# When block 2's memory is opened: at the third-last group of block 1, or at its last

## The chip, the cores and the metric

The kernel runs on one core of a Trainium2 chip. The metric is the device time of one execution in microseconds (us); where several runs are given, their median. The engines named below are PE (matrix multiply), DVE (vector), ACT (activation functions), POOL (a second, slower vector engine) and SP, whose queue issues nearly all DMA transfers.

## The reference

One transformer layer over 2048 positions of width 1024, in float32:

```
hn   = rms_norm(x, attn_norm_g);  proj = hn @ w_in        # q,k,v of 4 heads, gated linear attention, pooling
a    = diff_attention(q, k, v, lam, bias)                  # causal: block i of the queries sees keys 0..i
b, c = gated linear attention, multiscale pooling
h    = x + concat(a, b, c) @ w_out                         # output projection
hn   = rms_norm(h, ffn_norm_g)
out  = h + (silu(hn @ w_gate) * (hn @ w_up)) @ w_down      # FFN, hidden width 2816
```

## The kernel before

Every float32 matrix is split into a high and a low part, and each product is made of three matmuls (high by high, high by low, low by high). The positions are cut into four blocks of 512 (b = 0 to 3).

The first stage makes all projections and starts on attention. The second stage is the FFN, and it is the stage of this change. It walks over `steps`: for each block b, groups g = 0 to 10 (`NG` = 11), each group two slices of 128 of the hidden width (`GS` = 2). A group of blocks 0 and 1 is gate and up of its first slice (`first`, 48 matmuls of 512 columns), the down projection of the group before it (`down`, 48 matmuls), and gate and up of its second slice (`second`, 48 matmuls). The matmuls of `gate_up` and of `oproj` stand in `tile24`, at L1310 to L1312; those of `down` in the helper `mm`, at L133.

Blocks 2 and 3 do gate and up in another way. `unit` makes the product of a group by a scheme of seven products of half the size in place of eight (L1382, matmuls of 256 columns, 84 for a unit; a group has a unit "G" and a unit "U"). For that the normalised block has to be turned into seven operands first, named B11, T2, T1, B21, T3, B22 and T4, each in high and low parts. `tprep(b)` does this on DVE, ACT and POOL: it waits for the row scales of the block (`rowscale2`, which needs the last result of the output projection), normalises (L1245), forms sums and differences (L1250 to L1264), and splits them (L1239 on ACT, L1240 on DVE or POOL). The first products of a unit are made with B11, then T2, T1 and B21.

Beside this "left" stream of dense work runs a "right" stream, the attention of blocks 1 to 3 (`rside`). Both are Python generators; after each piece of dense work `tick` lets the right stream issue four steps (`RT2` = 4.0). So most of attention is issued between dense matmuls. At step (1, NG-3), group 8 of block 1, the line `until(lambda: not rside)` issues all that is left of attention in one piece. Only then its memory can be reused: the region `pp` is opened (one more weight buffer, three work buffers, half of block 2's rows), five more PSUM banks go to the dense stream, and block 2's mixed rows are loaded (`mixes(2)`) into X[2] and X[3], which held the keys and values of attention.

Weights pass through a ring of 2048-column buffers (`wring`; four of them in this stage until `pp` adds a fifth). `pieces` is the list of weight pieces in the order in which they are asked for, and `oplace` says at which step the output projection of a block stands: block 2's at (1, NG-1), before the gate and up of the last group of block 1.

The order that the code issues is not quite the order that runs: a scheduler in the build fixes each engine's order, by its own estimate, and moves independent work forward. Each engine then works through its list in order, so an instruction that waits holds up all behind it on that engine. SP's queue is in order as well.

Of the kernel before, what the change touches and what calls it, by code (L numbers as in the profile page):

```python
# [20 lines left out]
KT = D // P  # L21
BLK = 512
NB = S // BLK
NF = 2816 // P
# [3 lines left out]
GS = 2  # L28
# [59 lines left out]
def body(nc, tc, V, G, ACT, PE, DMA, A, banks, dram):  # L88
    side, rside = [], []
    rate = [0.0, 0.0]  # L90
    def spawn(g):

        if g is not None:
            side.append(g)
            advance([g], side)
# [41 lines left out]
    X = [C.view(4096, R) for i in range(4)]  # L137
# [288 lines left out]
    pieces = []  # L426
# [7 lines left out]
    NG = NF // GS  # L434
    steps = [(b, g) for b in range(NB) for g in range(NG)]

    def oplace(b, g):

        return {(0, 0): 0, (1, 0): 1, (1, NG - 1): 2, (2, 3): 3}.get((b, g))

    keep = {}

    def kept(k, i):

        if (k, i) not in keep:
            keep[k, i] = dram(f"wk{k}{i}", [P, 2048])
        return keep[k, i]

    def dpiece(b, fi):
        return (("d", b, fi), kept("d", fi), A["w_d"][fi], -2 if b else 0)  # L450

    for n, (b, g) in enumerate(steps):
        ob = oplace(b, g)
        if ob == 1:
            pieces += [dpiece(0, NF - GS + q) for q in range(2)]
        if ob is not None:
            pieces += [(("o", ob, d), kept("o", d), A["w_o"][d], -2 if ob else 0) for d in range(KT)]
        for i in range(2):
            if b < 2:
                fi = GS * g + i  # L460
                for k in "gu":
                    pieces.append(((k, b, fi), kept(k, fi) if b == 1 else None, A["w_" + k][fi], 0))
            else:
                pieces += [(("GU"[i], b, g), q, A[("w_g", "w_u")[i]][GS * g + q], -1) for q in range(2)]
            if i == 0 and n and ob != 1:
                pb, pg = steps[n - 1]
                pieces += [dpiece(pb, GS * pg + q) for q in range(2)]
    pieces += [dpiece(NB - 1, NF - GS + q) for q in range(2)]
# [618 lines left out]
    for si, (half, k, b) in enumerate(seq):  # L1087
        kind, i = UN[k]
# [25 lines left out]
        else:  # L1114
            n = 272 if i == 2 else 256
# [37 lines left out]
    fring = p2.ring(4, 1024, R)  # L1153
# [8 lines left out]
    def getw(key):  # L1162
        while key not in W2:
            pump()
            tick()
        return W2[key]

    def relw(key):
        wrel(W2.pop(key)[2])

    xs = [(r3(X[2 * q], KT), r3(X[2 * q + 1], KT)) for q in range(2)] + [None]
    ready = {}
# [285 lines left out]
    def down(b, g, ds):  # L1458
        grp = range(GS * g, GS * g + GS)
        dw = [getw(("d", b, fi)) for fi in grp]  # L1460
        for d in ds:
            until(lambda: all((fi, b) in fft for fi in grp))
            bank = force(dense.acq())
            prs = []
            for fi, (dH, dL, _) in zip(grp, dw):
                fH, fL, _ = fft[(fi, b)]
                prs += [(dH[:, d, :], fH), (dH[:, d, :], fL), (dL[:, d, :], fH)]
            mm(bank, prs)
            spawn(ch_down(d, b, bank, g == NG - 1))
            if d % 2:  # L1470
                pump()
            tick()
        if d == KT - 1:
            for fi in grp:
                fring.rel(fft.pop((fi, b))[2])
                relw(("d", b, fi))
# [17 lines left out]

    mixes(0)
    for n, (b, g) in enumerate(steps):
        if (b, g) == (1, NG - 3):
            until(lambda: not rside)
            dense.rel(*sbank.free, obank.free.pop())
            sbank.free.clear()  # L1500
            pp = Region(tc, "pp")
            wring.rel(pp.view(2048, R))
            tr2.rel(*[pp.view(528) for _ in range(3)])
            h2[2] = [pp.view(BLK) for _ in range(4)] + ht[4:8]
            acc2.append(pp.view(BLK))
            mixes(2)
        ob = oplace(b, g)
        if ob == 1:
            down(0, NG - 1, range(4))
        if ob is not None:  # L1510
            oproj(ob)
        if ob == 1:
            down(0, NG - 1, range(4, KT))
        if ob == 2:
            ready[("Xa", 2)] = True
            spawn(tprep(2))
        if (b, g) == (2, 1):
            until(lambda: ready.get(("Tall", 2)))
            mx = Region(tc, "mx", "right")
            xs[2] = (r3(mx.view(4096, R), KT), r3(mx.view(4096, R), KT))  # L1520
            mixes(3)
        if ob == 3:
            mx.close()
            lend()
        if (b, g) == (2, NG - 3):
            claim()
        if (b, g) == (2, NG - 1):
            until(lambda: len(back) == 3)
            wx.pop().close()
            spawn(tprep(3))  # L1530
        first(b, g)
        split = b != 1 and g == NG - 1
        if n and ob != 1:
            down(*steps[n - 1], range(4 if split else KT))
        second(b, g)
        if (b, g) == (1, NG - 1):
            ready[("Xb", 2)] = True
            fring.rel(X[1][:, 2048:3072], X[1][:, 3072:4096])
        if (b, g) == (2, NG - 1):
            ready[("Xa", 3)] = ready[("Xb", 3)] = True  # L1540
        if (b, g) == (0, NG - 1):
            mixes(1)
        if split:
            down(*steps[n - 1], range(4, KT))
# [85 lines left out]
```

## Time and profile before

| what | us |
|---|---|
| median of 3 runs (2691.2 to 2696.0) | 2693.79 |
| the profiled execution | 2695.36 |
| its span in the trace | 2693.6 |
| PE busy in the span | 2546.4 (95%) |
| DVE busy | 1932.9 (72%) |
| ACT busy | 1193.8 (44%) |
| POOL busy | 905.8 (34%) |

The profiled execution took 1.8 us beyond its span and is 1.6 us above the median. The page's second part cuts the span into 40 slices of 67 us and gives each engine's busy share in tenths, so one can see at once where PE is not full; a row below it gives the clock that PE was granted.

### The profile page before, as it was taken

The numbers are of one execution on the slowest core, as the hardware profiler recorded it, in microseconds if no ns is written. First come the engines' busy times: TensorE is split into PE (matmuls) and PEld (weight loads), VectorE is DVE, ScalarE is ACT, GpSimd is POOL, SyncE is SP. The second block draws the span as 40 slices with busy tenths as digits, with TensorE's granted clock in tenths as the row PEclk, the third lists the DMA queues.
The fourth block names the chain that finished last, engine by engine and source line by source line (L and its number), as shares of the span: only waits on it lengthen the run. The fifth ranks groups of instructions, "written<-read, shape, count | busy, mean of one in ns | idle before, by whom it ended". The sixth has DMA issues, their size and how long they took to land.

```text
span 2693.6 us, 39021 instructions
## 1 busy us (share of the span) xinstructions
PE 2546.4 (95%) x14064; PEld 2170.0 (81%) x14064; DVE 1932.9 (72%) x4002; ACT 1193.8 (44%) x2275; POOL 905.8 (34%) x595
## 2 busy tenths in 40 slices
PE   7998889989899999999999999779999999999999
PEld 5886778868778888877788887567788999899998
DVE  7769886689678787875767677752773678766665
ACT  3555645356554544444444354441342333433332
POOL 4326432355734343322322212011323332423332
PEclk8999989999999999999999999789999999999999
DMA  5333645336755545566776757327586665676664
GB/s 167 123 111 112 188 138 159 106 102 209 259 175 163 183 137 174 153 216 198 250 237 223 245 198 250 83 78 257 182 297 243 261 239 179 231 266 225 242 252 171
DMA packets 185518, 517.52 MB, mean 192 GB/s; under 512 B 19067, under 2 KB 63660, under 8 KB 158700
## 3 DMA queue, kind: packets, MB, share of 16 engines
q1 hardware_dynamic: 185036, 515.00, 56.8%
q8 instruction: 111, 1.82, 0.3%
q14 instruction: 83, 0.68, 0.1%
q10 hardware_dynamic: 288, 0.02, 0.0%
HBM read 386.10 MB, written 128.84 MB: 191 GB/s over the span
## 4 chain that ended last, share of the span: by engine, by line
PE 72%; DVE 16%; DMA 4%; issue 4%; ACT 3%; POOL 2%; SPq 0%; DVEq 0%; POOLq 0%; ACTq 0%
PE bk L133 29%; PE bk L1382 14%; PE bk L1312 7%; PE bk L1310 7%; PE bk L1311 7%; PE bk L1106 2%; PE bk L1107 2%; PE bk L1108 2%; PE bk L986 2%; DVE at L961 1%; DMA at<-qd 1%; DVE p L1347 1%; DVE c L249 1%; DVE at L941 1%; ACT at L953 1%
## 5 line engine op out<-in xcount | busy, mean ns | idle before, releaser
L133 PE MATMUL bk<-p,c 128*128 128x512 f32 x1184 | 323.2, 398 | 11.5 <-DVE p L217 3.9
L1310 PE MATMUL bk<-c,c 128*128 128x512 f32 x664 | 266.8, 403 | 5.6 <-DMA c<-wko 3.2
L1312 PE MATMUL bk<-c,c 128*128 128x512 f32 x664 | 265.3, 400 | 1.8 <-POOL c L542 1.7
L1311 PE MATMUL bk<-c,c 128*128 128x512 f32 x664 | 266.5, 402 | 0.0
L133 PEld LDWEIGHTS bk<-p,c 128*128 128x128 f32 x1184 | 218.0, 190 | 58.2 <-DVE p L217 4.3
L953 ACT ACTIVATE at<-at,at 128x1024 f32<-128x1024 f32 (+4 forms) x192 | 171.6, 895 | 172.0 <-DVE at L950 171.8
L542 POOL TENSOR_TENSOR c<-c,c 128x1024 fp32r<-128x1024 f32 x58 | 143.4, 2475 | 244.0 <-ACT c L541 198.0
L1347 DVE TENSOR_TENSOR p<-p,bk 128x512 f32<-128x512 f32 x308 | 203.6, 680 | 27.4 <-PE bk L133 26.8
L941 DVE TENSOR_SCALAR_CACHE_REDUCE at<-bk 128x512 f32<-128x512 f32 (+3 forms) x304 | 154.5, 521 | 93.8 <-PE bk L133 92.2
L133 PE MATMUL bk<-c,c 128*128 128x256 f32 (+2 forms) x1344 | 206.5, 302 | 9.3 <-DVE p L393 3.7
L133 PE MATMUL bk<-c,at 128*128 128x512 f32 (+4 forms) x704 | 188.2, 364 | 25.3 <-DMA at<-qd 12.4
L1106 PE MATMUL bk<-c,c 128*128 128x512 f32 x448 | 183.8, 412 | 18.9 <-ACT c L554 9.4
L1382 PE MATMUL bk<-c,c 128*128 128x256 f32 x1488 | 196.7, 283 | 4.0 <-POOL c L493 1.9
L133 PEld LDWEIGHTS bk<-c,c 128*128 128x128 f32 x1344 | 181.5, 190 | 20.6 <-DVE p L393 4.7
L1382 PEld LDWEIGHTS bk<-c,c 128*128 128x128 f32 x1488 | 187.9, 190 | 8.0 <-POOL c L493 2.3
L1107 PE MATMUL bk<-c,c 128*128 128x512 f32 x448 | 184.1, 411 | 5.9 <-DVE c L250 5.7
L1108 PE MATMUL bk<-c,c 128*128 128x512 f32 x448 | 182.0, 406 | 1.4 <-DVE c L555 1.4
L133 PEld LDWEIGHTS bk<-c,at 128*128 128x128 f32 x704 | 120.8, 195 | 57.2 <-DVE at L941 26.6
L1310 PEld LDWEIGHTS bk<-c,c 128*128 128x128 f32 x664 | 126.2, 190 | 35.6 <-DMA c<-wko 3.7
L1312 PEld LDWEIGHTS bk<-c,c 128*128 128x128 f32 x664 | 126.2, 190 | 31.0 <-POOL c L542 2.7
L1311 PEld LDWEIGHTS bk<-c,c 128*128 128x128 f32 x664 | 126.3, 190 | 28.1 <-DVE c L1182 0.3
L133 PE MATMUL bk<-at,c 128*128 128x256 f32 (+1 forms) x856 | 143.9, 289 | 1.9 <-DVE at L991 0.7
(378 smaller groups left out, 5912.9 us busy)
## 6 DMA issues: line engine op xcount, KB each, us to landing
c<-wkd SPq DMA_DIRECT2D x38, 1024.0 KB, 6.5
c<-w_u SPq DMA_DIRECT2D x56, 512.0 KB, 5.8
c<-w_g SPq DMA_DIRECT2D x55, 512.0 KB, 5.8
wkg<-c SPq DMA_DIRECT2D x19, 1024.0 KB, 4.9
c<-kd SPq DMA_DIRECT2D x72, 256.0 KB, 5.0
c<-vd SPq DMA_DIRECT2D x72, 256.0 KB, 3.9
c<-wko SPq DMA_DIRECT2D x17, 1024.0 KB, 5.4
p<-w_g SPq DMA_DIRECT2D x33, 512.0 KB, 5.3
```

The costliest lines, as they stand in the source:

```text
L133: PE.matmul(out, l, r, start=start and i == 0, stop=stop and i == n - 1)
L542: G.tensor_tensor(wL, raw[:, :1024], f(wH), op=ALU.subtract)
L941: V.tensor_scalar(p[:, c0:c0 + far], pt[:, :far], 1.0, None, op0=ALU.mult, op1=ALU.max, accum_out=mx[:, nx:nx + 1])
L953: ACT.activation(p[:, c0:c1], p[:, c0:c1], AF.Exp, bias=nmx, accum_out=u.z[:, i, m, k:k + 1])
L1106: PE.matmul(bank, wH[:, kt, :], hH[:, kt, :], start=st, stop=False)
L1107: PE.matmul(bank, wH[:, kt, :], hL[:, kt, :], start=False, stop=False)
L1108: PE.matmul(bank, wL[:, kt, :], hH[:, kt, :], start=False, stop=sp)
L1310: PE.matmul(bank, wH[:, kt, :], H[:, kt, :], start=st, stop=False)
L1311: PE.matmul(bank, wH[:, kt, :], L[:, kt, :], start=False, stop=False)
L1312: PE.matmul(bank, wL[:, kt, :], H[:, kt, :], start=False, stop=sp)
L1347: V.tensor_tensor(h2[b][d], h2[b][d], bank, op=ALU.add)
L1382: PE.matmul(out, l[:, k, :], r[:, k, :], start=start and k == 0 and n == 0, stop=k == 3 and n == 2, skip_group_check=True)
```

## The change

The opening of the memory (the `until`, the `pp` region, the banks, `mixes(2)`) moves from step (1, 8) to step (1, 10). Block 2's output projection moves from ahead of group 10 of block 1 to step (2, 0), behind group 10's gate and up. The down projection of group 10, which before stood between the units G and U of (2, 0), is now issued in one piece after the output projection and ahead of unit G. The list of weight pieces follows. Half of X[1] is given to the ring of FFN results at (2, 0), and X[0] and X[1] are declared free for the operands at the same place as X[2] and X[3].

```diff
-        return {(0, 0): 0, (1, 0): 1, (1, NG - 1): 2, (2, 3): 3}.get((b, g))
+        return {(0, 0): 0, (1, 0): 1, (2, 0): 2, (2, 3): 3}.get((b, g))
...
+        if ob == 2:
+            pieces += [dpiece(1, NF - GS + q) for q in range(2)]
...
-            if i == 0 and n and ob != 1:
+            if i == 0 and n and ob not in (1, 2):
...
-        if (b, g) == (1, NG - 3):
+        if (b, g) == (1, NG - 1):
             until(lambda: not rside)
...
         if ob == 2:
-            ready[("Xa", 2)] = True
+            ready[("Xa", 2)] = ready[("Xb", 2)] = True
+            fring.rel(X[1][:, 2048:3072], X[1][:, 3072:4096])
             spawn(tprep(2))
+            down(1, NG - 1, range(KT))
...
-        if n and ob != 1:
+        if n and ob not in (1, 2):
             down(*steps[n - 1], range(4 if split else KT))
         second(b, g)
-        if (b, g) == (1, NG - 1):
-            ready[("Xb", 2)] = True
-            fring.rel(X[1][:, 2048:3072], X[1][:, 3072:4096])
```

The new lines push the code down by two, so L1310 of before is L1312 of after, and so on.

What this does to PE's list is shown at two places. In the rows, bk is a PSUM bank; at is a buffer of attention; c3 and c4 are X[2] and X[3] (attention's keys and values, later block 2's mixed rows and operands); c1 is X[0]; p213, p214, c16 to c18 and pp1 hold weights; p215 to p218 hold FFN results.

First, PE in group 8 of block 1, behind the gate and up of its first slice. Before:

```order
L1312 MATMUL bk1_62<-c1_72,p213_6371 128x512
L133 MATMUL bk2_63<-p216_6374,c17_100 128x512 x3
L133 MATMUL bk2_63<-p217_6375,c18_101 128x512 x2
L133 MATMUL bk4_65<-c3_74,at31_9988 128x256 x2
L133 MATMUL bk3_64<-c3_74,at31_9988 128x512 x2
L133 MATMUL bk2_63<-p217_6375,c18_101 128x512
L133 MATMUL bk6_67<-c3_74,at31_9988 128x512 x2
L133 MATMUL bk5_66<-at316_10003,c10_83 128x256
L133 MATMUL bk5_66<-at317_10004,c10_83 128x256
L133 MATMUL bk4_65<-c3_74,at31_9988 128x256 x2
```

After:

```order
L1314 MATMUL bk1_62<-c1_72,p213_6371 128x512
L133 MATMUL bk2_63<-p216_6374,c17_100 128x512 x3
L133 MATMUL bk2_63<-p217_6375,c18_101 128x512 x3
L133 MATMUL bk0_61<-p216_6374,c17_100 128x512 x2
L133 MATMUL bk3_64<-c3_74,at31_9988 128x512 x2
L133 MATMUL bk4_65<-c3_74,at31_9988 128x256 x2
L133 MATMUL bk6_67<-c3_74,at31_9988 128x512 x2
L133 MATMUL bk0_61<-p216_6374,c17_100 128x512
L133 MATMUL bk0_61<-p217_6375,c18_101 128x512 x3
L133 MATMUL bk5_66<-at316_10003,c10_83 128x256
L133 MATMUL bk5_66<-at317_10004,c10_83 128x256
L133 MATMUL bk1_62<-p216_6374,c17_100 128x512 x3
```

Before, from the row with bk6 on, 424 matmuls of attention follow one another with no dense one between them. After, dense work stands between them, and the unbroken run begins only at the same place of group 10, with 276 matmuls; the other 148 stand among the dense matmuls of groups 8 and 9.

Second, PE at the first step of block 2. Before (the two last gate and up matmuls of block 1, then unit G, with `down` of group 10 between its products):

```order
L1311 MATMUL bk3_64<-c2_73,c16_99 128x512
L1312 MATMUL bk3_64<-c1_72,c16_99 128x512
L1382 MATMUL bk4_65<-c3_74,p213_6371 128x256 x12
L1382 MATMUL bk7_68<-c4_75,pp1_14566 128x256 x12
L1382 MATMUL bk6_67<-c3_74,c18_101 128x256
L1382 MATMUL bk4_65<-c4_75,p213_6371 128x256 x12
L133 MATMUL bk0_61<-p218_6376,c16_99 128x512 x3
L133 MATMUL bk1_62<-p218_6376,c16_99 128x512 x3
```

After (the last two matmuls of the output projection, `down` of group 10, the two matmuls for the row scales, in bank bk3 from c9, and the units G in bk4 and U in bk0):

```order
L1313 MATMUL bk5_66<-c4_75,c18_101 128x512
L1314 MATMUL bk5_66<-c3_74,c18_101 128x512
L133 MATMUL bk4_65<-p215_6373,pp1_14950 128x512 x3
L133 MATMUL bk4_65<-p218_6376,c16_99 128x512 x3
...
L133 MATMUL bk3_64<-p216_6374,c9_82 128x512 x2
L133 MATMUL bk3_64<-p215_6373,pp1_14950 128x512 x3
L133 MATMUL bk3_64<-p218_6376,c16_99 128x512 x3
L1384 MATMUL bk4_65<-c3_74,p213_6371 128x256
L1384 MATMUL bk0_61<-c3_74,c16_99 128x256
L1384 MATMUL bk4_65<-c3_74,p213_6371 128x256 x11
```

Between the end of the output projection and unit G stood a whole group's gate and up of one step, 96 matmuls, and 48 of `down`; now the 48 of `down` alone stand there.

## Rows read from the trace of the kernel before

**Rows 1.** The profile's page, second part: PE's busy share and PE's granted clock, in tenths, in 40 slices of 67 us.

```profile
PE   7998889989899999999999999779999999999999
...
PEclk8999989999999999999999999789999999999999
```

**Rows 2.** Windows: length, busy us of PE, PEld (PE's weight loads), DVE, ACT and POOL with instruction counts in brackets, the granted clock as a share of full speed, DMA's busy share and GB/s.

```profile
1663.70:1712.50 48.80, 33.76 (x144) 23.56 (x143) 36.93 (x125) 24.34 (x48) 3.40 (x4) 0.74 0.37 104
1712.50:1784.80 72.30, 53.36 (x283) 42.16 (x282) 50.48 (x160) 34.08 (x69) 3.88 (x6) 0.80 0.15 44
1784.80:1840.00 55.20, 47.74 (x199) 37.05 (x198) 26.41 (x45) 17.45 (x30) 11.52 (x7) 0.94 0.56 198
...
1840.00:1896.20 56.20, 56.20 (x242) 45.27 (x241) 10.83 (x17) 9.50 (x14) 12.41 (x8) 1.00 0.71 252
```

**Rows 3.** Waits between 1660 and 1800 us: who waited for whom, us in total, times, longest.

```profile
PEld bk L133 <- DVE at L941: 20.6, 18, 5.3
...
PE bk L133 <- DMA at<-qd: 9.7, 2, 4.9
```

**Rows 4.** Timeline of PE: the first matmul of attention's unbroken run, the 149th of the run, and the first dense matmul behind it. Columns: start, us taken, line, operation, count.

```profile
1663.69 0.63 PE L133 MATMUL bk<-c,at 128*128 128x512 f32 x2
...
1712.52 0.78 PE L133 MATMUL bk<-at,c 128*128 128x256 f32 x2
...
1784.84 0.39 PE L133 MATMUL bk<-p,c 128*128 128x512 f32 x1
```

**Rows 5.** Windows over four groups of block 1 ahead of the run (from the first gate matmul of a group to that of the next), counting only PE's matmuls of attention: length, busy us and count of these, granted clock, DMA. They follow one another from 1375.00 to 1553.30 us.

```profile
1375.00:1416.30 41.30, 9.72 (x67) 1.00 0.78 274
1416.30:1456.30 40.00, 8.47 (x34) 1.00 0.69 237
1456.30:1505.20 48.90, 19.35 (x106) 1.00 0.58 182
1505.20:1553.30 48.10, 15.80 (x105) 1.00 0.82 293
```

**Rows 6.** Windows, as rows 2, over the groups in which the attention of block 2's queries begins.

```profile
1266.40:1293.40 27.00, 23.86 (x129) 19.64 (x128) 22.70 (x48) 15.63 (x29) 11.20 (x8) 1.00 0.86 267
1293.40:1318.30 24.90, 21.79 (x91) 16.17 (x90) 17.23 (x53) 11.68 (x24) 9.90 (x7) 0.93 0.64 210
```

**Rows 7.** Timeline behind the run: SP's loads of the last three mixed rows into the new region, and PE's instructions that stood idle first (in square brackets: for how long, and for whom).

```profile
1808.14 1.62 SPq L1180 DMA_DIRECT2D pp<-mix  x3
...
1810.09 0.63 PE L1310 MATMUL bk<-c,pp 128*128 128x512 f32 x1 [2.34 <-ACT pp L541]
1813.46 5.40 PE L133 MATMUL bk<-p,c 128*128 128x512 f32 x15 [2.31 <-DMA c<-wkd]
...
1828.86 0.50 PE L1312 MATMUL bk<-c,c 128*128 128x512 f32 x1 [1.71 <-POOL c L542]
```

**Rows 8.** Timeline of PE behind the output projection of block 2, whose last matmul ended at 1896.2: `down`'s 48 matmuls, led by one for the row scales; the first product of unit G; and the product that waited.

```profile
1907.66 11.27 PE L133 MATMUL bk<-p,c 128*128 128x512 f32 x49
...
1929.97 1.57 PE L1382 MATMUL bk<-c,p 128*128 128x256 f32 x12
...
1937.08 2.93 PE L1382 MATMUL bk<-c,p 128*128 128x256 f32 x12 [3.19 <-ACT pp L1388]
```

**Rows 9.** Timeline of DVE in the same stretch: the last result of the output projection (L1193), the row scales (L202, L217, L1217), the first four of the eight normalisations (L1245), and the sums, differences and low parts of the operands (L1250; L1240 for B11 and B21; L1255 for T2; L1256; L1264; L1240 for the low part of T2).

```profile
1896.43 0.69 DVE L1193 TENSOR_TENSOR p<-bk,c 128x512 f32<-128x512 f32 x1 [4.91 <-PE bk L1312]
1901.03 0.43 DVE L202 CAST p<-pp 128x512 fp32r<-128x512 f32 x1 [3.91 <-POOL pp L1201]
...
1911.20 0.74 DVE L217 SCALAR_TENSOR_TENSOR c<-bk,c,c 128x512 f32<-128x512 f32 x1
...
1914.86 0.42 DVE L1217 TENSOR_SCALAR pp<-c 128x512 f32<-128x512 f32 x1
...
1915.79 2.73 DVE L1245 SCALAR_TENSOR_TENSOR tp<-pp,c,pp 128x512 f32<-128x512 f32 x4
...
1922.88 1.66 DVE L1250 TENSOR_TENSOR tp<-tp 128x1024 f32<-128x1024 f32 x1
...
1924.47 4.55 DVE L1240 TENSOR_TENSOR c<-tp,c 128x1024 fp32r<-128x1024 f32 x2
...
1929.55 2.82 DVE L1255 TENSOR_TENSOR tp<-tp,tp 128x1024 f32<-128x1024 f32 x1
1932.29 3.38 DVE L1256 TENSOR_TENSOR tp<-tp 128x1024 f32<-128x1024 f32 x1
...
1936.20 1.21 DVE L1264 TENSOR_TENSOR tp<-tp,tp 128x1024 f32<-128x1024 f32 x1
...
1938.53 1.22 DVE L1240 TENSOR_TENSOR c<-tp,c 128x1024 fp32r<-128x1024 f32 x1
```

**Rows 10.** Timeline of POOL in the same stretch: the last sum of squares (L1201), its low part (L203), a low part of a weight (L493), and the low parts of T1 and B22 (L1240).

```profile
1899.71 1.28 POOL L1201 TENSOR_TENSOR pp<-pp,pp 128x512 f32<-128x512 f32 x1
1901.53 1.29 POOL L203 TENSOR_TENSOR p<-pp,p 128x512 fp32r<-128x512 f32 x1 [0.54 <-DVE p L202]
...
1925.51 2.43 POOL L493 TENSOR_TENSOR pp<-c,pp 128x1024 fp32r<-128x1024 f32 x1 [2.05 <-ACT pp L492]
1927.90 6.69 POOL L1240 TENSOR_TENSOR c<-tp,c 128x1024 fp32r<-128x1024 f32 x2
```

**Rows 11.** DMA issues over the whole span: what, on which queue, count, KB each, median us from issue to landing. The first is a tile of raw up weights, the second a tile of the output projection's prepared weights.

```profile
c<-w_u SPq DMA_DIRECT2D x56, 512.0 KB, 5.8
...
c<-wko SPq DMA_DIRECT2D x17, 1024.0 KB, 5.4
```

## The prediction

> **What bounds the kernel now.** I read the page first: PE is full in nearly all slices, and the one deep dip, in busy share and in granted clock alike, stands near 1700 to 1830 us [rows 1]. That is the place of the change. The windows show the dip as the unbroken run of attention [rows 2, 4]: from 1663.69 to 1784.84 us PE has nothing but attention in its list, is busy for 87 of 121 us, and has a granted clock of 0.74 and 0.80, that is, part of the time the lower of its two levels. The waits of that stretch say why: PE waits for DVE, which takes the scores out of PSUM, and for the load of the next queries [rows 3]. Attention by itself is a chain from engine to engine, and nothing fills its gaps. Among dense matmuls it is otherwise: in four groups ahead of the run PE is as good as always busy at full clock, with 34 to 106 matmuls of attention in each [rows 5]. Behind the run comes a second, smaller loss: the first matmuls that need the new region wait for it [rows 7]. The third is at the start of block 2, where unit G waits for its operands [rows 8]. Only PE's time counts in these stages, so I price all in PE's time.
>
> **The change part by part.** Its work is the same, matmul for matmul; what changes is what stands beside what.
>
> *The run gets shorter.* By PE's lists it falls from 424 matmuls to 276. The 276 begin, in the trace of before, at 1712.52; so 1712.52 − 1663.69 = 48.8 us of run go away, and 72.3 us stay if the rest keeps its pace [rows 2, 4].
>
> *The 148 matmuls that leave the run.* They now stand in groups 8 and 9. Their price there: the four groups of rows 5 took 178.3 us with 312 matmuls of attention. A group has 144 dense matmuls of 0.23 us (11.27 / 49, rows 8), 33.1 us. So (178.3 − 4 × 33.1) / 312 = 0.147 us each, and 148 cost 21.8 us: +22. The 276 left in the run cost 0.26 each; that is why moving them pays. From both sides: the groups in which block 2's attention began were worse, with 6.2 of 51.9 us of PE idle [rows 6]; at that share two groups of some 45 us would lose another 10. The low end is the matmuls' bare price, no less than 20. I take 22, since rows 5 are the nearest in place and in mix.
>
> *Behind the run.* Before, PE had 48 gate and up and 42 `down` matmuls there to cover the opening of the region, and then lost 2.34 + 2.31 + 1.71 us in waits, and 15 matmuls took 5.40 us where 3.5 is the price at full clock, altogether some 8 us [rows 7]. After, its list has 42 `down`, 24 gate, and 24 of the output projection ahead of the first that needs the new buffer: the same 90 matmuls, so the first wait stays. The mixed rows that go through the new work buffers (issued at 1808.14 before, rows 7) are then needed by the output projection, but 24 up matmuls, 5.5 us, stand ahead. The weights behind that are the output projection's: they come ready from DRAM, so the wait for POOL's split (1.71) goes, and I see one wait where there were three: −3, between −5 and, if the loads are late, +5. The two groups' gate and up no longer run with eight banks but with three, as the groups of rows 5 do; that costs nothing there.
>
> *The start of block 2.* Here the change pays. The operands hang on the end of the output projection, and the cover shrinks from 96 + 48 to 48 matmuls, 11 us. I count from the last matmul of the output projection, in the order of after's lists. DVE's last sum ends at 0.9, POOL's last sum of squares at 4.9, since a weight's low part (2.43) stands ahead of it; rounding and low part add 0.4 and 1.3 [rows 9, 10]: 6.8. PE does the row-scale pair behind 42 of `down`, at 10.2. Three ACT steps and L217 took 3.1 from there in before (1908.1 to 1911.2): 13.3. But ahead of L217 DVE's list has the first step for unit U's weights, whose raw tile can be loaded only once POOL is done with its buffer, at 3.7, and lands 5.8 later [rows 11], at 9.5; with six more DVE steps of 0.6 behind it, L217 comes at 13.8. L217 to the end of L1217 took 4.1 with other work between, 1.8 without: 15.6. Eight normalisations of 0.67: 21. One result of `down` 0.6, the first difference 1.7, the low part of B11 1.2 to 3.3: **25**. PE has run out of work at 11.6, so 13.4 us idle. From there to the low part of T2 took 14 us before (from 1925.7, the end of the first L1240, to 1939.75), of which 2.4 were four DVE steps that are gone: 11.6 [rows 9]. In that time PE has four products of 1.4 (B11 for G and for U, B21, T1): 6 us idle more. Two more for waits on weights and 2 for matmuls at half clock behind the gaps (12 took 2.93 and not 1.57 behind a gap of 3.19, rows 8): 23 us. Before lost some 5 there (3.19, and 1.4 on the slow twelve). So **+18**, between +8, where DVE and POOL do not hinder each other, and +26, where all that before took from 1896.2 to 1939.75, 43.5 us, is seen but for 17 us of cover.
>
> DVE's 2.82 and 3.38 stand while POOL is busy (1927.90 to 1934.59), its 1.21 while POOL is idle [rows 9, 10]. The Trainium skill (SBUF — State Buffer, section "Who interferes with whom") speaks against the change here: a DVE operation that reads both its inputs from SBUF and a GpSimd operation that reads SBUF shut each other out for the whole instruction. By that rule the preparation is a series of both engines' operations, six of 1.2 and three of 2.4, some 3 us more than my 11.6, and the sum below would be −9 instead of −12. The rows agree as to the sign.
>
> *What else moves.* SP's queue keeps its order but for eight output-projection weights of 1 MB, which now are loaded behind the region's opening and not ahead of it. PE takes one in 24 × 0.23 = 5.5 us, a load lands in 5.4 [rows 11], and five buffers overlap them; the stretch behind the run moved 198 GB/s, the next 252 [rows 2]. I cost it at nothing; the cover is the buffers, and the last rival says what it costs without. `down` of group 10, out of the units' gaps, leaves unit U to follow G at once; the wait for U's weights is in the 2 us above.
>
> Sum: −48.8 + 22 − 3 + 18 = −11.8, or **−12 us**. The profiled execution is 2695.4, so 2683.6; it lies 1.6 above the median of before, so against 2693.8 I say **2682**.
>
> **The rivals.** (a) *The rest of the run does not keep its pace.* It now starts behind a group with other attention work under way, and the two groups may run as those of rows 6. For it: where the chain is cut is chance. Against: the windows on either side of 1712.5 are alike, 0.69 and 0.74 busy [rows 2]. Price: +10 in the groups, time 2692, which is no change.
> (b) *The stall at block 2 is small*, because the scheduler's list lets PE take parts of products as operands come (the list has U's first product between parts of G's) and little of the chain is contended: +8 instead of +18, time 2672.
> (c) *The gain is eaten, and more.* The output projection of block 2 starves for weights. It needs 8 × (1 MB + 0.26 MB of x) in 45 us, 235 GB/s, beside three mixed tiles and stored weights; before, five buffers were filled ahead. At 198 GB/s a step takes 6.6 us and not 5.5, +9 in all, time 2691; at 145 GB/s it takes 9 us, +28, time 2710. It decides from about 185 GB/s down, where the 12 us are used up. Against it: the next stretch had 252 [rows 2].
> (d) *The change does not do what it says*: if the run after were not shorter, all of +18 would show, near 2709. The lists speak against it.
>
> **How the numbers follow.** My forecast (run shorter by 45 to 52, block 2 later by 13 to 22) 0.55, with 2675 to 2688; (b) 0.18; (a) 0.14; (c) 0.10; (d) 0.03. About 0.2%, 5.4 us, is what a measurement of this kernel can tell from no change. The forecast is faster in 0.49 of its 0.55, else the same; (b) is faster; (a) the same but for 0.01 faster and 0.01 slower; (c) splits into 0.04 the same and 0.06 slower; (d) is slower. So faster 0.68, same 0.22, slower 0.10. The range leaves out about 1 in 10 at either side: 2665 to 2697.
>
> **What would show it.** In the profile of after: an unbroken run of attention of about 72 us (65 to 80) that starts near 1752 (1663.7 + 288 × 0.23 + 22); groups 8 and 9 with PE full, each some 11 us longer than one without attention; a gap of PE of 10 to 16 us in front of the first L1384, and a second of 4 to 8 before the first product with T2. I am wrong if the run is above 90 us, if PE waits for output-projection weights, or if the gaps at block 2 sum to under 10 or over 30 us.

## The result, and the profile after

The changed kernel takes 2676.65 us (median of 6 runs, 2667.9 to 2681.5); the kernel before, run beside it, 2693.11. The ratio is 0.9930, with an interval of 0.9912 to 0.9947. It is faster by 16.5 us where 12 were predicted. The profiled executions lie further apart, since they are 2.3 us above and 2.3 us below their medians: their spans are 2693.6 and 2672.5, 21.1 us.

To say where these 21 us are, I give each matmul in PE's list its price at full clock (0.233 us for 512 columns, 0.116 for 256, 0.085 for fewer, the distance of their starts where PE is full) and call the rest of a stretch its **loss**:

| stretch | before | after | predicted change |
|---|---|---|---|
| groups 8 and 9 and the run of attention | 66.3 | 36.8 | -48.8 + 22 = -27 |
| behind the run, to the end of the output projection | 10.3 | 1.5 | -3 |
| start of block 2, from there to the sixth unit | 13.4 | 31.6 | +18 |
| sum | 90.0 | 69.9 | -12 |

**The run.** Windows of after, counting only PE's matmuls of attention: group 8, group 9, and the unbroken run.

```profile
1638.40:1686.40 48.00, 17.22 (x103) 1.00 0.67 242
1686.40:1735.10 48.70, 18.74 (x105) 1.00 0.59 195
1750.40:1820.40 70.00, 50.92 (x276) 0.80 0.26 89
```

The run of 276 matmuls took 70.0 us, at 0.80 of the clock as before [rows 2]; the run of 424 took 121.2 [rows 4]. Groups 8 and 9 stay at full clock like those of [rows 5]: 96.7 us less two times 33.1 for their dense matmuls leaves 30.5 us for 208 matmuls of attention, 0.147 each, the price that the prediction took from [rows 5].

**Behind the run.** Windows of after (columns as in [rows 2]), then PE's first dense matmuls behind the run and the only two waits of PE of 0.1 us or more from there to the end of the output projection, then SP's loads.

```profile
1820.40:1840.00 19.60, 19.27 (x94) 15.86 (x93) 10.83 (x23) 6.03 (x14) 4.28 (x4) 1.00 0.28 95
1840.00:1879.00 39.00, 38.55 (x166) 30.79 (x165) 12.99 (x20) 8.06 (x13) 5.15 (x4) 1.00 0.88 313
1879.00:1911.00 32.00, 23.03 (x98) 18.01 (x96) 17.99 (x26) 6.89 (x9) 9.86 (x6) 0.95 0.59 197
1911.00:1936.00 25.00, 15.54 (x96) 15.34 (x97) 16.31 (x17) 10.41 (x14) 15.65 (x4) 0.73 0.23 78
```

```profile
1820.52 1.54 PE L133 MATMUL bk<-p,c 128*128 128x512 f32 x6
...
1839.65 0.50 PE L1312 MATMUL bk<-c,c 128*128 128x512 f32 x1 [0.33 <-DMA c<-wko]
...
1845.46 0.49 PE L1313 MATMUL bk<-c,p 128*128 128x512 f32 x1 [0.45 <-DVE c L1184]
```

```profile
1840.25 1.39 SPq L1182 DMA_DIRECT2D pp<-mix  x3
1843.43 1.00 SPq L586 DMA_DIRECT2D c<-wko  x2
```

The mixed rows go into the region from 1840.25 on, 20 us behind the run's end, and the dense matmuls cover that but for these two waits. The three waits of [rows 7] are gone. The first of them was for the split of a raw weight into the new buffer (ACT at L541, POOL at L542). ACT of before; then ACT, POOL and PE of after at the same weight:

```profile
1806.18 1.05 ACT L541 CAST p<-c 128x1024 fp32r<-128x1024 f32 x1 [6.14 <-PE bk L1311]
...
1809.00 1.03 ACT L541 CAST pp<-c 128x1024 fp32r<-128x1024 f32 x1
```

```profile
1832.56 1.03 ACT L543 CAST pp<-c 128x1024 fp32r<-128x1024 f32 x1
...
1835.65 2.39 POOL L544 TENSOR_TENSOR pp<-c,pp 128x1024 fp32r<-128x1024 f32 x1
...
1843.92 0.40 PE L1312 MATMUL bk<-c,pp 128*128 128x512 f32 x1
```

After, too, the first weight through the new buffer is a raw one. Before, it stood in ACT's list behind the split of another raw weight, which waited 6.14 us for PE, and ACT reached it at 1809.00, when PE was waiting already (since 1807.75). After, nothing of that kind stands ahead of it, and it is ready at 1838.0, 5.9 us before PE takes it. DMA moves 313 GB/s from 1840 to 1879, where most of the output projection runs (252 in [rows 2]), and PE does not starve.

**The start of block 2.** PE of after, from the last matmul of the output projection (columns as in [rows 8]); then DVE (L217 and L1219 the row scales, L1247 the normalisations, L1252 the first difference, L1257 and L1258 the next sums, L1242 low parts); then POOL (L495 a weight's low part, L1242 the low parts of T1 and B22).

```profile
1889.20 0.40 PE L1314 MATMUL bk<-c,c 128*128 128x512 f32 x1
...
1902.53 0.95 PE L133 MATMUL bk<-p,pp 128*128 128x512 f32 x3 [2.95 <-DVE c L217]
...
1909.76 0.58 PE L1384 MATMUL bk<-c,p 128*128 128x256 f32 x1 [5.58 <-ACT c L1241]
...
1914.20 2.71 PE L1384 MATMUL bk<-c,p 128*128 128x256 f32 x11 [3.65 <-DVE c L1242]
...
1926.64 2.50 PE L1384 MATMUL bk<-c,pp 128*128 128x256 f32 x10 [6.27 <-POOL c L1242]
```

```profile
1901.72 0.75 DVE L217 SCALAR_TENSOR_TENSOR c<-bk,c,c 128x512 f32<-128x512 f32 x1 [0.23 <-ACT c L216]
...
1908.55 2.73 DVE L1247 SCALAR_TENSOR_TENSOR tp<-p,c,pp 128x512 f32<-128x512 f32 x4
...
1911.80 1.21 DVE L1252 TENSOR_TENSOR tp<-tp 128x1024 f32<-128x1024 f32 x1
1912.93 2.35 DVE L1242 TENSOR_TENSOR c<-tp,c 128x1024 fp32r<-128x1024 f32 x2
1915.20 1.21 DVE L1257 TENSOR_TENSOR tp<-tp,tp 128x1024 f32<-128x1024 f32 x1
1916.34 1.21 DVE L1258 TENSOR_TENSOR tp<-tp 128x1024 f32<-128x1024 f32 x1
...
1918.61 3.48 DVE L1242 TENSOR_TENSOR c<-tp,c 128x1024 fp32r<-128x1024 f32 x3
```

```profile
1904.41 2.34 POOL L495 TENSOR_TENSOR pp<-c,pp 128x1024 fp32r<-128x1024 f32 x1 [8.31 <-ACT pp L494]
1913.38 10.91 POOL L1242 TENSOR_TENSOR c<-tp,c 128x1024 fp32r<-128x1024 f32 x1 [6.62 <-ACT c L1241]
1924.25 2.34 POOL L1242 TENSOR_TENSOR c<-tp,c 128x1024 fp32r<-128x1024 f32 x1
```

Four gaps of PE, 18.5 us in all, and half clock behind them (11 matmuls of 256 columns in 2.71 us; twelve took 1.57 in [rows 8]). The first three, 12.2 us, wait for the chain of operand B11; the fourth waits for the low part of T1 on POOL. POOL's two operations took 13.2 us, the first of them 10.91, while DVE worked on without a pause. The first is B22's: it began at 1913.38, when T1 itself was made (L1252, done at 1913.01) but not yet rounded (1.04 us on ACT). T1's low part stood behind it and ended at 1926.59, and PE goes on at 1926.64. In [rows 9] and [rows 10] the same pair met the other way round: POOL 6.69 for its two, and DVE's operations up to 3.38 for one that takes 1.21 after.

### The profile page after: what moved, and what is told of

Its sections match the earlier page's. It is cut to its first block, busy times and chain, and to the rows that moved or that the text cites. A ratio compares the mean times of both kernels' runs of the same rounds, so it can differ in the third digit from the quotient of the medians.

```text
span 2672.5 us, 38997 instructions
## 1 busy us (share of the span) xinstructions
PE 2537.2 (95%) x14064; PEld 2170.1 (81%) x14064; DVE 1939.9 (73%) x4002; ACT 1192.2 (45%) x2275; POOL 911.0 (34%) x595
## 4 chain that ended last, share of the span: by engine, by line
PE 74%; DVE 14%; issue 4%; DMA 3%; ACT 3%; POOL 2%; SPq 0%; DVEq 0%; POOLq 0%; ACTq 0%
PE bk L133 30%; PE bk L1384 14%; PE bk L1313 7%; PE bk L1314 7%; PE bk L1312 7%; PE bk L1108 2%; PE bk L1109 2%; PE bk L1110 2%; PE bk L988 2%; DVE at L963 1%; DVE c L250 1%; DVE c L249 1%; DMA at<-qd 1%; ACT at L955 1%; DVE at L943 1%
## 5 line engine op out<-in xcount | busy, mean ns | idle before, releaser
L133 PE MATMUL bk<-p,c 128*128 128x512 f32 x1136 | 312.2, 399 | 9.9 <-DVE p L217 3.9
L1312 PE MATMUL bk<-c,c 128*128 128x512 f32 x680 | 272.8, 402 | 3.5 <-DMA c<-wko 3.5
L1313 PE MATMUL bk<-c,c 128*128 128x512 f32 x680 | 272.5, 401 | 0.0
L1314 PE MATMUL bk<-c,c 128*128 128x512 f32 x680 | 270.9, 399 | 0.1
L133 PEld LDWEIGHTS bk<-p,c 128*128 128x128 f32 x1136 | 209.3, 190 | 53.5 <-DVE p L217 4.3
L1384 PE MATMUL bk<-c,c 128*128 128x256 f32 x1824 | 239.6, 283 | 0.3 <-ACT c L1390 0.3
L544 POOL TENSOR_TENSOR c<-c,c 128x1024 fp32r<-128x1024 f32 x61 | 151.3, 2483 | 258.8 <-ACT c L543 231.2
L1384 PEld LDWEIGHTS bk<-c,c 128*128 128x128 f32 x1824 | 230.2, 190 | 4.5 <-ACT c L1390 0.7
L1108 PE MATMUL bk<-c,c 128*128 128x512 f32 x448 | 185.1, 415 | 18.6 <-ACT c L556 9.4
L133 PE MATMUL bk<-c,c 128*128 128x256 f32 (+2 forms) x1272 | 184.2, 297 | 6.3 <-DVE p L393 3.1
L1109 PE MATMUL bk<-c,c 128*128 128x512 f32 x448 | 184.5, 412 | 5.2 <-DVE c L250 5.2
L1110 PE MATMUL bk<-c,c 128*128 128x512 f32 x448 | 183.0, 408 | 1.4 <-DVE c L557 1.4
L133 PEld LDWEIGHTS bk<-c,c 128*128 128x128 f32 x1272 | 168.5, 190 | 14.9 <-DVE p L393 4.5
L1312 PEld LDWEIGHTS bk<-c,c 128*128 128x128 f32 x680 | 129.0, 190 | 33.2 <-DMA c<-wko 4.2
L1314 PEld LDWEIGHTS bk<-c,c 128*128 128x128 f32 x680 | 128.8, 189 | 29.3 <-POOL c L544 0.5
L1313 PEld LDWEIGHTS bk<-c,c 128*128 128x128 f32 x680 | 129.1, 190 | 28.8 <-DVE c L1184 0.3
```

The source lines that it names most:

```text
L133: PE.matmul(out, l, r, start=start and i == 0, stop=stop and i == n - 1)
L544: G.tensor_tensor(wL, raw[:, :1024], f(wH), op=ALU.subtract)
L1108: PE.matmul(bank, wH[:, kt, :], hH[:, kt, :], start=st, stop=False)
L1109: PE.matmul(bank, wH[:, kt, :], hL[:, kt, :], start=False, stop=False)
L1110: PE.matmul(bank, wL[:, kt, :], hH[:, kt, :], start=False, stop=sp)
L1312: PE.matmul(bank, wH[:, kt, :], H[:, kt, :], start=st, stop=False)
```

## The experiments

The table gives all of them; each ratio is to the kernel before, run beside them. Loss is as above, from the profiled execution; that of before lies some 3 us above its median, so its loss does too.

| kernel | opened at | output projection | us | ratio (interval) | loss around and behind the run | loss, start of block 2 |
|---|---|---|---|---|---|---|
| before | group 8 | ahead of group 10 | 2691.9 to 2693.1 | 1 | 76.6 | 13.4 |
| changed | group 10 | behind group 10 | 2676.65 | 0.9930 (0.9912 to 0.9947) | 38.3 | 31.6 |
| after_again | group 10 | behind group 10 | 2676.2 | 0.9939 (0.9925 to 0.9954) | 40.7 | 32.6 |
| e1 | group 10 | ahead of group 10 | 2670.06 | 0.9915 (0.9898 to 0.9931) | 53.6 | 10.6 |
| e2 | group 8 | behind group 10 | 2712.67 | 1.0073 (1.0055 to 1.0092) | 76.8 | 30.2 |
| e3 | as changed, low parts on DVE | | 2676.12 | 0.9935 (0.9919 to 0.9951) | 38.2 | 29.1 |
| e5 | group 9 | ahead of group 10 | 2670.94 | 0.9917 (0.9901 to 0.9934) | 54.9 | 10.6 |
| e15 | as e5, low parts on DVE | | 2670.38 | 0.9919 (0.9906 to 0.9932) | 54.7 | 10.9 |
| e10 | group 7 | ahead of group 10 | 2709.45 | 1.0058 (1.0044 to 1.0073) | 91.4 | 11.6 |
| e9 | group 10 | inside group 10 | 2673.61 | 0.9928 (0.9913 to 0.9943) | 46.1 | 22.8 |
| e13 | group 10 | ahead, `down` of 9 before it | 2677.44 | 0.9941 (0.9925 to 0.9956) | 50.1 | 21.4 |
| e14 | as e13, `down` of 10 ahead of G | | 2681.98 | 0.9965 (0.9953 to 0.9977) | 50.7 | 26.3 |
| e17 | as e14, low parts on DVE | | 2681.77 | 0.9959 (0.9948 to 0.9971) | 49.8 | 25.5 |

**The theory** is the prediction's: the gain is the shorter run, and the price is paid at block 2, for the cover that is lost there. Its rivals: the late opening itself makes the stall, or the cut's place in attention's chain makes the gain. The first two kernels take the change apart.

**e1**: the kernel before with the opening moved, and nothing else.

```diff
-        if (b, g) == (1, NG - 3):
+        if (b, g) == (1, NG - 1):
             until(lambda: not rside)
```

> The kernel before with the memory opened at the last group of block 1 and nothing else: block 2's output projection stays ahead of that group's gate and up. If the gain is the shorter run and the cost the lost cover at block 2, then this keeps the gain and has no cost: run as in the changed kernel (around it some 30 us less lost than before), block 2's start as before (no more than 15 us of PE lost between the end of the output projection and the first products), but the output projection stands right behind the run, with new buffers, weights and mixed rows not yet loaded, so up to 10 us are lost there: 2662 to 2675, below the changed kernel. The rival, that what stands behind the run sets the time (the mixed rows and prepared weights are loaded late wherever the output projection follows the opening at once), says that 20 us or more are lost there and the time is 2680 or above.

PE of e1 where the output projection first needs a mixed row in the new region, and SP's load of these rows:

```profile
1839.53 0.80 PE L1310 MATMUL bk<-c,c 128*128 128x512 f32 x1 [4.39 <-ACT c L1181]
```

```profile
1836.11 1.34 SPq L1180 DMA_DIRECT2D pp<-mix  x3
```

2670.06, below the changed kernel. The start of block 2 costs as before, so the late opening does not make the stall. Around and behind the run e1 loses 53.6, 15 us more than the changed kernel, where up to 10 were expected: the first matmuls of the output projection stand among the last attention, whose gaps they don't fill, and then PE waits for a mixed row that needs the new region and was issued only at 1836.11.

**e2**: the other half alone, the changed kernel with the opening back at (1, NG-3).

```diff
-        if (b, g) == (1, NG - 1):
+        if (b, g) == (1, NG - 3):
             until(lambda: not rside)
```

> The other half alone: the changed kernel with the memory opened at the third-last group again (run of 424 matmuls as before), block 2's output projection still behind the last group's gate and up. If the shrunken cover (48 matmuls of down in place of 96 + 48) causes the stall at the start of block 2, it shows here with all of its size, since nothing is loaded late: 18 us more than before less 0 to 5 for a smoother stretch behind the run, 2705 to 2713. The rival, that the late opening (late loads of mixed rows and weights) causes that stall, says as before, 2690 to 2697.

Waits of PE in e2, behind the run and at the start of block 2:

```profile
1807.33 0.80 PE L1312 MATMUL bk<-c,pp 128*128 128x512 f32 x1 [2.34 <-ACT pp L543]
...
1939.50 1.07 PE L133 MATMUL bk<-p,p 128*128 128x512 f32 x3 [2.88 <-DVE c L217]
...
1946.74 0.58 PE L1384 MATMUL bk<-c,c 128*128 128x256 f32 x1 [4.88 <-ACT c L1241]
...
1951.18 4.21 PE L1384 MATMUL bk<-c,c 128*128 128x256 f32 x18 [2.59 <-DVE c L1242]
...
1963.62 1.65 PE L1384 MATMUL bk<-c,p 128*128 128x256 f32 x6 [5.20 <-POOL c L1242]
```

20 us slower than before, as the theory said, with the same four gaps as after, 15.6 us. The stall belongs to the move of the output projection. The halves are -22.6 and +20.0; together they gave -16.5 and not -2.6. The move pays 15 us back only where the opening is late, since the work that it leaves behind the run then covers the opening.

**e5 and e10**: the kernel before with the opening one group later, and one earlier.

```diff
-        if (b, g) == (1, NG - 3):
+        if (b, g) == (1, NG - 2):      # e5;  e10: NG - 4
             until(lambda: not rside)
```

> The kernel before with the memory opened one group later in place of two, the output projection where it was before. By the price of attention's matmuls (0.26 us in the run, 0.147 among dense work) the run is 25 us shorter and 85 matmuls that leave it cost 12.5, so -12.7; the stretch behind the run and the start of block 2 have all the cover that they had before: 2676 to 2684 by this sum. If behind the run the same losses vanish as in the changed kernel (some 9 us), 2669 to 2674. The rival, that the gain does not go with the length of the run but with where its cut falls in attention's chain, says any time between 2665 and 2695 with a run that is not 25 us shorter.

> The kernel before with the memory opened one group earlier, everything else as it was: the unbroken run of attention has 521 matmuls and not 424. The opening one later took 85 matmuls out of the run and 12 to 13 us off the loss around it, 0.15 us a matmul. If the length of the run is the price, 97 more cost some 15 us: 2702 to 2712 with a loss around the run near 80 us. The rival, that the place of the cut in attention's chain sets the loss, says a loss around the run that is not near 80, anywhere in 2680 to 2702 or above 2712.

Windows over the run of e5 and of e10, and PE's first waits behind it in each:

```profile
1706.48:1802.00 95.52, 67.98 (x340) 52.39 (x339) 67.26 (x214) 44.90 (x90) 5.77 (x9) 0.75 0.23 62
```

```profile
1618.80:1765.20 146.40, 103.68 (x522) 80.16 (x521) 101.77 (x329) 67.18 (x134) 9.74 (x13) 0.78 0.31 89
```

```profile
1821.17 0.49 PE L1310 MATMUL bk<-c,c 128*128 128x512 f32 x1 [0.35 <-DMA c<-wko]
...
1826.39 0.73 PE L1310 MATMUL bk<-c,c 128*128 128x512 f32 x2 [0.32 <-ACT c L1181]
```

```profile
1790.51 0.50 PE L1310 MATMUL bk<-c,pp 128*128 128x512 f32 x1 [2.34 <-ACT pp L541]
1793.59 5.77 PE L133 MATMUL bk<-p,p 128*128 128x512 f32 x15 [2.34 <-DMA p<-wkd]
```

e5 takes 2670.94, as expected if the losses behind the run vanish too, and e10 2709.45, within the range of the theory. Runs of 521, 424, 339 and 276 matmuls took 146.4, 121.2, 95.5 and 70.0 us, 0.25 to 0.29 each wherever the cut falls, and lost 78.7, 66.3, 53.3 and 36.8 (with the groups ahead of them): the length sets the loss. Behind the run e10 loses 12.7 and has the waits of before [rows 7], e5 loses 1.6. Both have the same 90 dense matmuls of cover; what differs is the weights around the one that comes first through the new buffer, a raw one in all four kernels. In e10, as in before, ACT splits two other raw weights between the run's end and this one (at 1779.40 and, after 6.15 us of waiting for PE, at 1786.61; the new buffer's at 1789.43). In e5, as in after, it has none: the new buffer's is split at 1814.00, and the weights that follow are the output projection's, prepared. e2, opened where before is, has the first wait of [rows 7] too (2.34).

**e3 and e15**: the low parts of T1 and B22 of block 2 on DVE, in the changed kernel and in e5.

```diff
-        hl("T1", T1, G)
+        hl("T1", T1, V if b == 2 else G)
...
-        hl("B22", b22, G)
+        hl("B22", b22, V if b == 2 else G)
```

> The changed kernel with the low parts of two operands of block 2 (T1 and B22) made by DVE in place of POOL. In the changed kernel the second gap of the start of block 2 (6.27 us) ends with POOL's low part, which took 13.2 us for two while DVE worked without a pause. If the contention between POOL and DVE makes that gap, it goes: the low part of T1 is there about 1.2 us after its turn on DVE, and the start of block 2 loses 4 to 6 us less: 2669 to 2674 against 2676.7. The rival, that DVE's own list is what is late (each low part that it takes over delays T2, B21 and what follows by 1.2 us), says that the later operands wait instead and the time stays within 2 us of the changed kernel.

> The kernel with the memory opened one group later (2670.9 before), with the low parts of T1 and B22 of block 2 made by DVE and not by POOL. Here the cover ahead of unit G is whole, and the operand that is waited for is T2, which DVE makes while POOL works on those low parts (2.8 and 3.4 us for operations that take 1.2 alone). If that contention sets the wait, DVE's two operations are 3.8 us shorter, its two added ones of 1.2 come behind T2, and the start of block 2 loses 3 to 4 us less than the 10.7 of the kernel without this edit: 2666 to 2669. The rival, as in the same edit on the changed kernel, is that another operand is then late: 2670 to 2672, a loss there of 9 us or more.

DVE's step behind T2 in e5 and in e15, then a wait of PE in e15 and four in e3:

```profile
1904.68 3.42 DVE L1256 TENSOR_TENSOR tp<-tp 128x1024 f32<-128x1024 f32 x1
```

```profile
1907.69 1.21 DVE L1256 TENSOR_TENSOR tp<-tp 128x1024 f32<-128x1024 f32 x1
```

```profile
1915.58 5.98 PE L133 MATMUL bk<-p,pp 128*128 128x512 f32 x18 [1.90 <-DMA pp<-wkd]
```

```profile
1901.98 0.97 PE L133 MATMUL bk<-p,pp 128*128 128x512 f32 x3 [2.95 <-DVE c L217]
...
1909.23 0.58 PE L1384 MATMUL bk<-c,p 128*128 128x256 f32 x1 [5.60 <-ACT c L1241]
...
1913.67 2.72 PE L1384 MATMUL bk<-c,p 128*128 128x256 f32 x11 [3.64 <-DVE c L1242]
...
1930.35 2.30 PE L1384 MATMUL bk<-c,c 128*128 128x256 f32 x12 [2.22 <-ACT pp L1414]
```

No change in time, twice. The contention does go (3.42 becomes 1.21), and in e3 the 6.27 us wait for POOL with it, but other waits come up behind it: the start of block 2 loses 29.1 and not 31.6 in e3, 10.9 and not 10.6 in e15. In e3 the three gaps of B11's chain stay. Up to the 85th matmul of the units it loses 15.1 us where the changed kernel loses 23.6, but from there to the sixth unit 14 where the changed kernel loses 8. Its later waits name splits of weights (ACT at L494, POOL at L495) and steps of the units' results (ACT at L1414 and L1390), so what is saved early is given back behind. The rival held in the time; that DVE's longer list is the reason is not shown.

**e9**: the output projection inside group 10, between its `down` and its second gate and up, and the last `down` in one piece ahead of unit G (the weight list follows).

```diff
         first(b, g)
         if n and ob != 1 and (b, g) != (2, 0):
             down(*steps[n - 1], range(4 if split else KT))
+        if ob == 2:
+            oproj(2)
+            ready[("Xa", 2)] = True
+            spawn(tprep(2))
         second(b, g)
```

> The memory opened at the last group of block 1, as in the changed kernel, but the output projection of block 2 between that group's down projection and its second gate and up: 42 matmuls of down in front of the output projection cover the opening, and 48 of gate and up and 48 of down stand behind it, in front of the units (48 in the changed kernel). If each matmul of cover hides its own 0.23 us of the preparation, the start of block 2 loses 11 us less than in the changed kernel, and the stretch behind the run some 5 more: 2668 to 2673, a little below the changed kernel's 2676.7. The rival, that the preparation is slow whenever DVE, POOL and the loads work on it together and does not shrink with cover, leaves all of the stall: 2677 to 2684.

PE of e9 at the opening, and at the first unit product:

```profile
1845.13 0.80 PE L1314 MATMUL bk<-c,c 128*128 128x512 f32 x1 [4.28 <-DMA c<-wko]
...
1914.65 0.55 PE L1386 MATMUL bk<-c,p 128*128 128x256 f32 x1 [4.99 <-ACT c L1243]
```

2673.61, just above the range of the theory and below that of the rival. With 48 more matmuls (11 us) ahead of unit G the start of block 2 loses 9 us less than in the changed kernel; with 48 fewer behind the run, that stretch loses 8 more, 4.28 of it in a wait for weights. Cover works nearly one for one, and moving it from one place to the other gains little.

**e13, e14 and e17**: `down` of group 9 moved from behind the output projection to ahead of it (e13); besides, the last `down` ahead of unit G (e14); besides, the edit of e3 (e17). The weight list follows.

```diff
+        if ob == 2:
+            down(1, NG - 2, range(KT))
         if ob is not None:
             oproj(ob)
...
+        if (b, g) == (2, 0):                    # e14, e17
+            down(1, NG - 1, range(KT))
         first(b, g)
```

> The memory opened at the last group of block 1, then the down projection of the group before, then the output projection, then that whole group's gate and up. By the accounts of the runs so far: loss around the run as in the changed kernel (35 to 37 us), start of block 2 as in the kernel with the opening alone moved (some 11 us), and behind the run, where only some 30 matmuls of down stand between the opening and the output projection, between 2 (as in the changed kernel) and 17 us (as with the opening alone moved): 49 to 65 us in all against 90 before, 2652 to 2668, middle 2660, below every kernel so far. The rival, that the output projection behind the opening waits for weights and rows whatever stands ahead, gives the time of the opening alone moved, 2670.

> The kernel of the last batch that put the down projection between the opening and the output projection, with the last group's own down projection issued in one piece ahead of unit G and not between the units. That kernel lost 50 us around and behind the run and 21 at the start of block 2, although 111 dense matmuls stood ahead of the first unit product; its list held back 33 of the 48 of down behind the first unit products. If what counts is how many dense matmuls stand ahead of unit G in PE's list, then with all 144 there the start loses some 11 us, as in the kernels with the output projection where it was: 61 in all, 2662 to 2669. The rival, that the operands come late in that kernel for another reason (loads and the split of weights crowd DVE and POOL while the output projection ends), keeps most of the 21 us: 2673 to 2680.

> Both edits of the other two kernels of this batch together: all dense work ahead of unit G, and the low parts of T1 and B22 on DVE. If both do what they are meant to, the loss at the start of block 2 is some 7 us and the time 2659 to 2665, the shortest of all; if neither, 2673 to 2680.

PE of e14 in the last `down`, then DVE (L1259 and L1260 make operands of the units, L1340 is a step of the FFN result that `down` waits for) and ACT (L1345, which rounds that result):

```profile
1901.73 4.01 PE L133 MATMUL bk<-p,pp 128*128 128x512 f32 x17
1919.73 7.11 PE L133 MATMUL bk<-p,c 128*128 128x512 f32 x24 [13.98 <-ACT p L1345]
```

```profile
1904.99 3.38 DVE L1259 TENSOR_TENSOR tp<-tp,tp 128x1024 f32<-128x1024 f32 x1
1908.30 3.36 DVE L1260 TENSOR_TENSOR tp<-tp 128x1024 f32<-128x1024 f32 x1
1911.58 2.83 DVE L1340 TENSOR_TENSOR c<-c,c 128x512 f32<-128x512 f32 x1
```

```profile
1919.06 0.62 ACT L1345 CAST p<-c 128x512 fp32r<-128x512 f32 x1 [1.83 <-DVE c L1341]
```

My count of matmuls failed here. All 144 stand ahead of unit G in e14, and PE still idles 14 us, in the cover itself: the last 24 matmuls of `down` of group 10 need the result of the last gate and up, and DVE makes that result behind the operands of the units (L1259, L1260). In e1 and e5 the `down` in the cover is group 9's, whose inputs were long there, and the last group's stands among the units. e17 shows the same 25 us. e13 loses 21 us at block 2; there the first unit products stand ahead of most of that `down` and wait themselves. None of the three beats e1. e13 and e14 took longer than either theory said of them, so the rivals fail in their numbers too; e14's said rightly that the operands' preparation crowds DVE, but not that the cover itself would wait for it.

**after_again**: the changed kernel beside e9, e13 and e10.

> The changed kernel again, word for word, on the chip and beside the runs of the kernel before that the other three kernels of this batch share, so that they can be compared with it directly: 2676.7 within 3 us.

2676.2, as the first time.

## Why the prediction was right

*The run gets shorter, and the 148 matmuls that leave it*: right, in sign, place and size. The run starts at 1750.4 (near 1752 predicted) and takes 70.0 us (72); 0.147 us a matmul in groups 8 and 9 is what was forecast. Together -29.5 against -27. e5 and e10 show that the length is the cause. Rival (a) did not come about: the rest of the run kept its pace, 0.25 us a matmul where 0.26 was taken. One sign was off: groups 8 and 9 took 15 us more than a group without attention and not 11, since 60 of their 208 matmuls of attention stood there before.

*Behind the run*: the sign was right, the term mis-sized: -3 was predicted, -9 measured. Of the 8 us by which the losses pass the sum (-20.1 against -12), 6 are this term's. The step that failed is "the same 90 matmuls, so the first wait stays". The first wait of [rows 7] names ACT at L541, the split of a raw weight, and not the opening of the region; that name was in the row. After, ACT makes that split 11 us before PE takes the weight, and the wait is gone. e5 and e10, with equal cover, lose 1.6 and 12.7. That the raw weights ahead on ACT are the reason is read from the waits and the order of the splits in those kernels; no run exchanged the weights alone.

*The start of block 2*: +18 predicted, +18.2 measured, and e2 shows alone that it belongs to the output projection's move (+16.8 there). The two sides fit as well: up to the 85th matmul of the units before loses 5.3 us and after 23.6, where the forecast had 5 and 23; what is lost from there to the sixth unit is the same in both (8). The chain to B11 was 24.7 us (the first low part ends near 1914.1, the last matmul of the output projection at 1889.4) against 25. The gap ahead of the first L1384 was split: 2.95 for the row scales, 5.58 for B11's rounding and 3.65 for its low part, 12.2 together (13.4 predicted, but in front of the first product, where only 8.5 stand, so the gap of 10 to 16 us that was named as a sign did not show). The second gap was 6.27 us, within 4 to 8, but its reason was another: it was to be T2 on DVE, and it was T1's low part on POOL. The forecast took the contention of [rows 9] and [rows 10], in which DVE was the slowed side, as it stood; after, the same operations met with POOL as the slowed side. So size and place were right, and the last operand of the chain was wrong; that its wait came out at the same size is luck.

The Trainium skill (SBUF — State Buffer, section "Who interferes with whom") says that such a pair shuts each other out and that the order of issue decides who waits. The rows agree that it can fall either way: DVE 3.42 and 1.21 for one operation with POOL's low parts and without (e5, e15), POOL 13.2 us for two operations in after and 6.69 in before. By that rule the chain was to be 3 us longer and the gain smaller; e3 and e15 take the contention away, at the price of two more operations on DVE, and change the time by nothing that can be measured, so no run shows it as a term of the sum.

*The rivals.* (b), a small stall of 8 us, and (d) are wrong by the losses above. (c) did not come about: 0.33 us of waits for output-projection weights behind the run, at 313 GB/s. Such a wait showed in e9, e13 and e14 instead, once in each (4.2 to 4.3 us), where 42 matmuls or fewer separate the opening from the output projection.

What stays open: e1, e5 and e15 stand at 2670 to 2671, the changed kernel at 2676; their intervals against the kernel before overlap. But 10 of the changed kernel's 12 runs are longer than the longest of e1 (2673.34), and the losses (64 to 66 against 70 to 73) point the same way, so these 6 us are more than scatter, though the two were not run side by side. If so, half of the change, or one group of it, gives more than the whole. What keeps e3 from gaining behind its first units is open too.

## What to carry to other kernels

A stretch of dense work that needs nothing new is worth its own length wherever something else must be waited for, once: moving it from one gap to another gains only if the old gap has cover to spare. Take the two halves of such a change apart before keeping both. And count a matmul as cover only if its own inputs are ready without the engine that is late; a `down` whose input DVE makes behind the late operands waited 14 us with them.

## What I had not expected of the hardware

One POOL operation took 10.91 us beside a DVE that ran one SBUF-to-SBUF operation after another for 10.3 us (1911.80 to 1922.1), each in its usual 1.21. The next one of the same form took 2.34 us once DVE had paused. The first ended 2.2 us behind DVE's last, near the 2.34 that one takes alone. This fits a POOL that got next to nothing until DVE paused; the trace shows its start and end, not what it did between. Elsewhere (e14: POOL 3.02 to 3.35, DVE 2.83 to 3.38) the two took turns. What decides between turns and lock-out was not tried.
